# Thirty-two experts as one pipeline written in program order, a quarter of the weight subtractions on GpSimd

## The chip, the cores and the metric

The kernel runs on one core of a Trainium2 chip. The metric is the device time of one execution in microseconds (us), the median of several runs. Engines are named as the profile names them: PE (TensorE, matrix products), DVE (VectorE), ACT (ScalarE), POOL (GpSimd), SP (SyncE, which issues the loads).

## The reference

Three transformer blocks work one after the other on 512 tokens of 1024 features, in float32. The change touches only the third, and in it the mixture of experts:

```python
def clamped_swiglu_expert(xb, w_gu, b_gu, w_dn, b_dn):
    gu = xb @ w_gu + b_gu
    gate = jnp.minimum(gu[:, :D_FF_3], SWIGLU_LIMIT)
    up = jnp.clip(gu[:, D_FF_3:], -SWIGLU_LIMIT, SWIGLU_LIMIT)
    glu = gate * jax.nn.sigmoid(SWIGLU_ALPHA * gate)
    return ((up + 1.0) * glu) @ w_dn + b_dn
```

A router picks 4 of 32 experts for each token; each expert has 1024 x 2048 gate-and-up weights and 1024 x 1024 down weights, 12.58 MB together. The outputs of a token's four experts are summed, weighted by their gates. After the experts come a norm, a gate over a per-token embedding and a last norm.

## The kernel before

Blocks one and two fill the first 1900 us and stay as they are. In the third block `Moe.route` (L1423) finds each token's experts, and `Moe.run` (L1546) goes through the 32 experts. An expert has 96 slots (`CAP`) for its tokens.

**Exact products.** Every weight block, 128 x 2048 numbers (1 MB), is loaded by SP (`wblock`, L100, DMA at L92), copied by ACT into a rounded high part `wh` (L97), and DVE subtracts that from the block for a low part `wo` (L98). A product is then three matmuls (`mm3`, L163 to L167): high by high, high by low, low by high. An expert has 8 blocks of gate-and-up and 4 of down weights, each with 12 matmuls of 512 columns, so 144 matmuls, 12 copies on ACT and 12 subtractions on DVE. A load takes 512 columns of 512 rows of the matrix, so it reads runs of 2 KB.

**The rows of x.** `picked` (L1510) fetches and transposes an expert's tokens in one step: a matmul with a 0/1 matrix `hot` (L1516), for 3 experts at a time (`GRP`), over both parts of x, 64 matmuls per 3 experts. `places` (L1489) computes each slot's token, gate and target row, `chosen` (L1504) marks `hot` for a group.

**One expert.** `up` (L1610) opens an accumulator with the bias, a matmul over 64 rows (`bgu` has the two parts of the bias of 32 experts, L1617), then takes two blocks into it, and does this four times; `glu` (L1530) runs after each gate/up pair; `turn` (L1519) transposes a half of the hidden values; `down` (L1627) takes the four down blocks, ACT scales the result by the gate (L1639), and POOL adds the rows to the sum in DRAM by an indirect DMA (`add_rows`, L1722). Half 1 of an expert's `up` comes after the `down` of the one before. A scheduler orders the instructions of each engine.

**Buffers.** In the expert stage there are 5 tiles for loads, 3 for high parts, 3 for low parts. PSUM banks: 4 `gemm`, 3 `aux`, 1 `hold`.

**After the experts** `ple` (L1753) takes the sums back, with a bias matmul over 64 rows for each of 8 gate products (L1795).

Of the kernel before, what the change touches and what calls it, by code (L numbers as in the profile page):

```python
# [11 lines left out]
F32 = mybir.dt.float32  # L12
# [19 lines left out]
class Env:  # L32
    BANKS = {"gemm": 4, "aux": 3, "hold": 1}

    def __init__(self, ctx, tc):
        self.tc, self.nc = tc, tc.nc
        nc = self.nc
        self.cst = ctx.enter_context(tc.tile_pool(name="cst", bufs=1))
# [3 lines left out]
        self.psp = ctx.enter_context(tc.tile_pool(name="ps", bufs=4, space=bass.MemoryType.PSUM))  # L42
# [5 lines left out]
        self.n = 0  # L48
# [11 lines left out]
    def widen(self, ctx, slots, **more):  # L60
# [18 lines left out]

    def ps(self, s, tag="aux"):  # L80
# [24 lines left out]
    def split(self, hi, lo, src, scale=None):  # L105
        """src * scale into two float32r parts."""
# [8 lines left out]
    def bank(self, ctx, n):  # L115
        """n tiles [128, 4, 512] on the right until ctx closes."""
# [20 lines left out]
    def give(self, *tiles):  # L137
        """What was read for the last time."""
# [6 lines left out]
    def lend(self, n):  # L145
        """n more tiles each for the two parts of weights; returns what ends that."""
# [22 lines left out]
    def gemm_tok(self, xs, K, w, c0, cn, consume, eng=None):  # L169
        """Token-major: consume(tt, col, n, psum) for psum[tok, col:col+n] = x @ w[:, col:col+n]."""  # L170
# [52 lines left out]
    def bcast(self, pool, src, n, tag):  # L223
        """A row of n values in DRAM onto all partitions."""
# [4 lines left out]
    def transpose_in(self, xs, t, src, k=KT):  # L229
        """src [tok of tile t, k*128 features] into the feature-major pairs xs."""  # L230
# [8 lines left out]
    def rstd(self, pool, ssq, n, eps, tag):  # L239
        """(ssq / n + eps) ** -0.5 of a few columns."""  # L240
# [8 lines left out]
    def rms(self, pool, x, gain, eps, out, scratch=None):  # L249
        """out = x * rsqrt(mean(x^2) + eps) * gain of one token tile [128, 1024]."""  # L250
# [6 lines left out]
    def layer_norm(self, pool, x, eps, out, gain, bias, tag=""):  # L257
        """out = (x - mean) * rstd * gain + bias of one token tile [128, 1024]."""
# [17 lines left out]
def block1(e, a, res, more):  # L276
    """The first block's x, and what the second's first product takes."""
# [17 lines left out]
    with ExitStack() as ph:  # L295
# [8 lines left out]
        # -------- i_k, i_w, m_i, m_f in one stationary block  # L304
# [33 lines left out]
        # index keys: norm over the 64 features, on both partition halves  # L338
# [24 lines left out]
        # relative bias: strips of 256 keys per head, less the value of far keys  # L363
# [23 lines left out]
        # causal mask inside one tile of 128 keys: 0 where key <= query  # L387
# [11 lines left out]
        # -------- mLSTM gates, a head per partition  # L399
# [37 lines left out]
        # selectors of a head's row: pairs of 64 partitions, and all 128  # L437
# [9 lines left out]
        # token-major columns of c, the key weights and the floor of the denominator  # L447
# [11 lines left out]
        # 0 where key <= query within one chunk of 64, keys on partitions  # L459
# [39 lines left out]
        # -------- attention over the chosen keys, a head at a time, in three steps  # L499
# [50 lines left out]
        def attend(n0, n1):  # L550
            """Heads n0 to n1 of all 32, each step behind the one before it."""
# [11 lines left out]
        # -------- q, k of the mLSTM: causal conv over 4 tokens and silu  # L563
# [30 lines left out]
        # -------- mLSTM chunks  # L594
# [96 lines left out]
    # -------- ffn: conv of 3 tokens over both halves, silu(gate) * val  # L691
# [79 lines left out]
class Hidden:  # L771
    """Feature tiles [128, 512] of a ffn's hidden layer, four to a slot but the first ones."""
# [5 lines left out]
    def parts(self):  # L778
        """Of each slot: its first feature tile, how many, the slot."""
# [8 lines left out]
class Modulated:  # L788
    """layer_norm(x) * scale + shift, token tile by token tile, as a feature-major operand."""
# [13 lines left out]
class Ada:  # L803
    """silu(c) @ w_ada + b_ada, by columns of 512; the row goes to DRAM."""
# [34 lines left out]
def down(e, hd, w, add, done):  # L839
    """add(t, cols, psum) of hidden @ w, all eight accumulators open at once, then done(t)."""  # L840
# [41 lines left out]
def block2(e, a, u, res):  # L882
    """The second block's x, and the same feature-major, from e.xsp and its modulated norm u."""
# [5 lines left out]
    with ExitStack() as ph:  # L889
# [7 lines left out]
        # lower bounds: softmax over the two rows of logits, a head's features per column  # L897
# [16 lines left out]
        # 1 where key <= query within one chunk, keys on partitions  # L914
# [22 lines left out]
        for g in range(2):  # L937
# [35 lines left out]
            def prepare(j):  # L973
# [7 lines left out]
                # queries against the chunk's start and against their sub-chunk's  # L981
# [9 lines left out]
                # keys against each sub-chunk's start, and against the chunk's end  # L991
# [69 lines left out]
    with ExitStack() as ph:  # L1061
# [16 lines left out]
        # the first half where the gates of the first heads were  # L1078
# [33 lines left out]
        # -------- gates, projections, and the sum that w_out takes  # L1112
# [143 lines left out]
# tokens of an expert in the first pass, and experts whose tokens are picked at once  # L1256
# [15 lines left out]


def mixer3(e, a, x, xt, moe):
    """x = layer_norm(alpha * x + mixers), routed."""
    nc, tc = e.nc, e.tc
    with ExitStack() as ph:
# [3 lines left out]
        # taps and scales of a feature per partition  # L1281
# [586 lines left out]
```

## Time and profile before

| | |
|---|---|
| median of 3 runs | 3298.11 us (3297.29 to 3299.51) |
| the profiled execution: span of its instructions | 3294.7 us |
| PE busy, share of the span | 3222.8 us, 98% |
| DVE, ACT, POOL busy | 65%, 47%, 8% |
| DMA rate in the expert stage, GB/s | 307 to 363 by slices of 30 us |
| first bias matmul of expert 0 | 1939.35 us |
| last down matmul of expert 31 starts | 3206.79 us |

The span is the time from the first to the last instruction of the profiled execution, 3.4 us less than the median of the runs. Busy times of engines overlap; a busy engine is only the limit where it doesn't wait. A PE row's duration is longer than the distance to the next row, since matmuls are pipelined: the distance between starts is what a matmul costs.

### The profile page before, as it was taken

To read this page: it belongs to the slowest core of one execution; us is meant where nothing else is said; L and a number is where in the kernel's file an instruction comes from. 1 tells how busy PE (TensorE), PEld (TensorE's weight loads), DVE (VectorE), ACT (ScalarE), POOL (GpSimd) and SP (SyncE) were. 2 spreads that over 40 slices of the span, in tenths; PEclk is the share of its full clock that TensorE was granted. 3 is DMA by queue.
4 is the path that set the end of the run, shared out by engine and by line. 5 is a ranking of instruction groups with operands and counts; after the bars stand their busy time and mean duration, and the time that the engine had idled before them with its cause. 6 is when DMAs were issued, how large, how long until landed. Compare 5 with 4: busy or idle time off the path is not lost. (4 is left out here: it accounts for less than half of the span.)

```text
span 3294.7 us, 37481 instructions
## 1 busy us (share of the span) xinstructions
PE 3222.8 (98%) x15051; PEld 2434.6 (74%) x15051; DVE 2128.5 (65%) x2381; ACT 1564.5 (47%) x1655; POOL 272.7 (8%) x203
## 2 busy tenths in 40 slices
PE   7999999999999999999999999999999999999997
PEld 6776877878777788788778776666666666666665
DVE  5854687444636523822335778788888788888786
ACT  5343333323625223222322347777677667766662
POOL 2310011101000000200000100000000000000001
PEclk9997999999999999999999999999999999999999
DMA  4211465333222333232232259999999999999992
GB/s 143 77 39 62 147 218 201 115 109 97 64 64 64 89 113 122 87 109 92 83 119 90 91 204 330 332 324 319 330 329 329 327 327 325 323 331 325 328 328 104
DMA packets 324081, 626.96 MB, mean 190 GB/s; under 512 B 25144, under 2 KB 32672, under 8 KB 323834
## 3 DMA queue, kind: packets, MB, share of 16 engines
q1 hardware_dynamic: 320314, 611.89, 54.2%
q0 software_dynamic: 3584, 12.58, 1.9%
q8 instruction: 120, 1.97, 0.2%
q14 instruction: 63, 0.52, 0.0%
HBM read 603.43 MB, written 21.01 MB: 190 GB/s over the span
## 5 line engine op out<-in xcount | busy, mean ns | idle before, releaser
L98 DVE TENSOR_TENSOR wo<-wl,wh 128x2048 fp32r<-128x2048 f32 (+2 forms) x531 | 1190.3, 2254 | 627.8 <-ACT wh L97 625.8
L97 ACT ACTIVATE wh<-wl 128x2048 fp32r<-128x2048 f32 (+2 forms) x537 | 1009.0, 1885 | 744.6 <-PE pf L167 319.1
L165 PE MATMUL pf<-ah,wh 128*128 128x512 f32 (+1 forms) x1520 | 563.4, 371 | 0.6 <-ACT wh L97 0.6
L166 PE MATMUL pf<-ah,wo 128*128 128x512 f32 (+1 forms) x1520 | 562.2, 370 | 1.2 <-DVE wo L98 1.2
L167 PE MATMUL pf<-al,wh 128*128 128x512 f32 (+1 forms) x1520 | 561.5, 370 | 0.0
L165 PEld LDWEIGHTS pf<-ah,wh 128*128 128x128 f32 x1520 | 287.4, 189 | 56.4 <-ACT cy L727 6.9
L166 PEld LDWEIGHTS pf<-ah,wo 128*128 128x128 f32 x1520 | 287.0, 189 | 51.4 <-DVE wo L98 1.4
L167 PEld LDWEIGHTS pf<-al,wh 128*128 128x128 f32 x1520 | 286.5, 189 | 51.7 <-issue 3.7
L165 PE MATMUL pgu<-wh,xe 128*96 128x512 f32 x784 | 316.7, 404 | 0.0
L167 PE MATMUL pgu<-wo,xe 128*96 128x512 f32 x784 | 310.1, 396 | 1.8 <-DVE wo L98 1.7
L166 PE MATMUL pgu<-wh,xe 128*96 128x512 f32 x784 | 310.3, 396 | 0.0
L166 PE MATMUL pd<-wh,h 128*96 128x512 f32 x512 | 201.9, 394 | 0.0
L165 PE MATMUL pd<-wh,h 128*96 128x512 f32 x512 | 201.9, 394 | 0.0
L167 PE MATMUL pd<-wo,h 128*96 128x512 f32 x512 | 201.5, 393 | 0.1
L1722 POOL DMA_INDIRECT yd<-y,dst x32 | 79.1, 2472 | 1212.1 <-ACT y L1639 1112.1
L165 PEld LDWEIGHTS pgu<-wh,xe 128*96 128x96 f32 x784 | 126.3, 161 | 69.3 <-issue 22.2
L167 PEld LDWEIGHTS pgu<-wo,xe 128*96 128x96 f32 x784 | 126.6, 161 | 57.6 <-DVE wo L98 6.0
L166 PEld LDWEIGHTS pgu<-wh,xe 128*96 128x96 f32 x784 | 126.7, 162 | 45.9
L165 PE MATMUL pa<-wh,ah 128*128 128x512 f32 x352 | 143.0, 406 | 0.0
L167 PE MATMUL pa<-wo,ah 128*128 128x512 f32 x352 | 141.5, 402 | 0.2 <-DVE wo L98 0.2
L166 PE MATMUL pa<-wh,al 128*128 128x512 f32 x352 | 141.7, 402 | 0.0
L165 PE MATMUL pdn<-wh,ah 128*128 128x512 f32 x352 | 139.1, 396 | 0.7 <-ACT wh L97 0.7
(484 smaller groups left out, 4615.2 us busy)
## 6 DMA issues: line engine op xcount, KB each, us to landing
wl<-w_gate_up SPq DMA_DIRECT2D x256, 1024.0 KB
wl<-w_down SPq DMA_DIRECT2D x138, 1024.0 KB
wl<-w_in SPq DMA_DIRECT2D x54, 1024.0 KB
wl<-w_ada SPq DMA_DIRECT2D x24, 1024.0 KB
wl<-w_up SPq DMA_DIRECT2D x20, 1024.0 KB
wl<-w_ffn_in SPq DMA_DIRECT2D x20, 1024.0 KB
wl<-w_out SPq DMA_DIRECT2D x12, 1024.0 KB
wl<-w_ffn_out SPq DMA_DIRECT2D x10, 1024.0 KB
```

Of the source, the lines that this page charges most:

```text
L97: nc.scalar.activation(hi[:, :nk, :n], land[:, :nk, :n], AF.Copy)
L98: (eng or nc.vector).tensor_tensor(lo[:, :nk, :n], land[:, :nk, :n], hi[:, :nk, :n].bitcast(F32), op=ALU.subtract)
L165: mm(out, st[0], mv[0], start=first, stop=False)
L166: mm(out, st[1], mv[0], start=False, stop=False)
L167: mm(out, st[0], mv[1], start=False, stop=last)
L1722: self.e.nc.gpsimd.indirect_dma_start(out=self.yd, out_offset=bass.IndirectOffsetOnAxis(ap=dst[:, :1], axis=0), in_=y, in_offset=None, com ...
```

## The change

- The weights come in blocks of 128 whole rows (8 KB runs), the down weights by pairs of rows, also 8 KB; still 1 MB each. Loads are issued 7 blocks ahead, and copies and subtractions 3 blocks ahead (L1621 to L1630 of the changed kernel).
- Of the 12 subtractions of an expert, 9 stay on DVE and 3 go to POOL (`n % 4 == 1`, L1629): blocks 1 and 5 of gate-and-up and block 1 of down.
- A block now feeds all four gate/up accumulators, which are open together; their four bias matmuls (L1580) stand at the expert's start and use all 128 rows, as `sel` has zeros for the rest.
- `picked` is gone, and the two parts of x with it. `fetch` (L1549) computes the places and POOL gathers the 96 rows of x from DRAM by an indirect DMA (L1561), two experts ahead; `turn` transposes them, 8 more transposes per expert, with a copy on ACT and a subtraction on DVE for each four.
- The order is by program on every engine (`manual_schedule`): expert i's 8 wide blocks, the 4 narrow ones of expert i - 1, and so on; `glu` does both halves at once behind wide block 7.
- Rings: 5 tiles for loads, 4 high, 4 low. PSUM: 4 `gemm`, 2 `aux`, 2 `hold`. `ple` has its own pool, and its gate bias uses 128 rows.

```diff
-        self.sel = cp.tile([P, E], F32R, name="sel")
+        self.sel = cp.tile([P, E + 1], F32R, name="sel")
+        pick = tmp.tile([P, E + 1], F32, tag="pick", name="pick", bufs=1)
+        nc.gpsimd.memset(pick, 0.0)
...
     def room(self, ctx):
-        self.e.widen(ctx, 2, wh=1, wo=1)
+        self.e.widen(ctx, wl=2, wh=2, wo=2)
...
     def run(self, out):
...
+        e.layout(gemm=4, aux=2, hold=2)
...
+        def fetch(i):
...
+            pi, *took[i] = self.places(hots[p][:, :, j, :], self.tge[:, :, i, :])
+            src = wp.tile([P, 1], I32, tag="src", name=e.name("src"))[:CAP, :]
+            nc.vector.tensor_copy(src, pi[:, 0:1])
+            rows[i] = mp.tile([P, D], F32, tag="xg", name=e.name("xg"))[:CAP, :]
+            nc.gpsimd.indirect_dma_start(out=rows[i], out_offset=None, in_=self.xd,
+                                         in_offset=bass.IndirectOffsetOnAxis(ap=src[:, :1], axis=0))
...
+        def turn_x(i, g):
+            if i < N_EXP:
+                xs[i, g] = self.turn(rows[i][:, g * 512:(g + 1) * 512], entry("xe", 4))
+
+        def turn_h(i):
+            hs[i] = [self.turn(g, entry("h", 4), 1.0 / SW, 2) for g in gs.pop(i)]
+
+        def tops(i):
+
+            acc[i] = [e.ps("pgu", "gemm")[:CAP, :] for _ in range(4)]
+            for c in range(4):
+                nc.tensor.matmul(acc[i][c], self.sel[:, i:i + 1].to_broadcast([P, CAP]),
+                                 self.bgu[:, c * 512:(c + 1) * 512], start=True, stop=False)
+
+        def wide(i, k):
+            xh, xl = xs[i, k // 4]
+            hi, lo = tiles.pop(0)
+            for c in (0, 2, 1, 3):
+                e.mm3(acc[i][c], (xh[:, k % 4, :], xl[:, k % 4, :]), (hi[:, c, :], lo[:, c, :]), False, k == KT - 1)
...
+        def halve(n):
+            if n < len(steps):
+                land, hi, lo = lands.pop(0), e.ring("wh", F32R), e.ring("wo", F32R)
+                nc.scalar.activation(hi, land, AF.Copy)
+                eng = nc.gpsimd if n % 4 == 1 else nc.vector
+                eng.tensor_tensor(lo, land, hi.bitcast(F32), op=ALU.subtract)
+                tiles.append((hi, lo))
...
+        ahead, loaded = 3, 7
+        with tc.manual_schedule():
...
+            for n, (step, i, k, _) in enumerate(steps):
+                load(n + loaded)
+                halve(n + ahead)
+                if step is wide and k == 0:
+                    tops(i)
+                step(i, k)
+                if step is wide:
+                    if k == 2:
+                        fetch(i + 2)
+                    elif k in (4, 5):
+                        turn_x(i + 1, k - 4)
+                    elif k == KT - 1:
+                        gs[i] = self.glu(*[(acc[i][f], acc[i][2 + f]) for f in range(2)])
+                elif k == 3:
+                    ends(i)
+                    if i + 1 < N_EXP:
+                        turn_h(i + 1)
```

**PE, an expert's bias.** Here PE stands at an accumulator's bias in the kernel before (`pgu` is an accumulator, `xe` and `spot` hold rows of x, `pt` takes transposes):

```order
L167 MATMUL pgu_16253<-wo_16258,xe_15224 96x512
L165 MATMUL pgu_16253<-wh_16275,spot 96x512
L166 MATMUL pgu_16253<-wh_16275,spot 96x512
L1617 MATMUL pgu_16291<-bgu,sel 96x512
L1525 MATMUL pt_16336<-ident,g_16247 128x96 x4
L167 MATMUL pgu_16253<-wo_16276,spot 96x512
L165 MATMUL pgu_16253<-wh_16275,spot 96x512
```

and here at the start of an expert in the changed one:

```order
L1515 MATMUL pt_16364<-ident,g_16267 128x96 x4
L1580 MATMUL pgu_16377<-bgu,sel 96x512
L1580 MATMUL pgu_16378<-bgu,sel 96x512
L1580 MATMUL pgu_16379<-bgu,sel 96x512
L1580 MATMUL pgu_16380<-bgu,sel 96x512
L166 MATMUL pgu_16377<-wh_16299,xe_16195 96x512
L167 MATMUL pgu_16377<-wh_16299,xe_16195 96x512
L168 MATMUL pgu_16377<-wo_16300,xe_16195 96x512
L166 MATMUL pgu_16379<-wh_16299,xe_16195 96x512
```

The four bias matmuls stand in a row, a block's high part is then used for one accumulator after the other, and the picks of x (L1516) have gone from PE; four transposes stand in their place twice per expert.

**DVE, one expert.** In the kernel before DVE goes through an expert so (`g`, `u` are the gate products, `h` the transposed hidden values):

```order
L98 TENSOR_TENSOR wo_16349<-wl_16346,wh_16348 128x2048
L1538 TENSOR_SCALAR u_16332<-pgu_16291 96x512
L1539 SCALAR_TENSOR_TENSOR g_16329<-u_16332,g_16329 96x512
L98 TENSOR_TENSOR wo_16367<-wl_16364,wh_16366 128x2048
L98 TENSOR_TENSOR wo_16385<-wl_16382,wh_16384 128x2048
L98 TENSOR_TENSOR wo_16403<-wl_16400,wh_16402 128x2048
L113 SCALAR_TENSOR_TENSOR h_16421<-pt_16422,h_16421 128x384
L98 TENSOR_TENSOR wo_16476<-wl_16473,wh_16475 128x2048
L98 TENSOR_TENSOR wo_16494<-wl_16491,wh_16493 128x2048
```

and in the changed one, from `fetch`'s places to the gate products:

```order
L1498 TENSOR_TENSOR dst_16442<-free_16440,pi_16433 96x1
L1559 CAST src_16444<-pi_16433 96x1
L1629 TENSOR_TENSOR wo_16451<-wl_16333,wh_16450 128x2048
L1629 TENSOR_TENSOR wo_16469<-wl_16371,wh_16468 128x2048
L111 TENSOR_TENSOR xe_16484<-pt_16485,xe_16484 128x384
L1629 TENSOR_TENSOR wo_16495<-wl_16397,wh_16494 128x2048
L111 TENSOR_TENSOR xe_16510<-pt_16511,xe_16510 128x384
L1629 TENSOR_TENSOR wo_16539<-wl_16448,wh_16538 128x2048
L1527 TENSOR_SCALAR g_16554<-pgu_16377 96x512
L1527 TENSOR_SCALAR g_16556<-pgu_16378 96x512
L1532 TENSOR_SCALAR u_16560<-pgu_16379 96x512
```

The first subtraction here is wide block 6's, the one behind the second transposed half of x (`xe`, L111) narrow block 2's; those of wide block 5 and narrow block 1, which come just before them in the program, are POOL's. `glu`'s six instructions stand together, and two of them (L1534) read two operands from SBUF, as every subtraction does.

**POOL, the expert stage.** Before, POOL has one instruction per expert, the indirect add (L1722). In the changed kernel a stretch of it reads (`xg` are gathered rows, `yd` the sums):

```order
L1747 DMA yd<-y_14324,dst_13333 640x1024
L1629 TENSOR_TENSOR wo_14391<-wl_14288,wh_14390 128x2048
L1561 DMA xg_14419<-x3d,src_14417 96x1024
L1629 TENSOR_TENSOR wo_14494<-wl_14388,wh_14493 128x2048
L1629 TENSOR_TENSOR wo_14580<-wl_14491,wh_14579 128x2048
L1747 DMA yd<-y_14613,dst_13546 640x1024
L1629 TENSOR_TENSOR wo_14680<-wl_14577,wh_14679 128x2048
```

Per expert POOL now has three subtractions of a block, a gather and the add.

## Rows read from the trace of the kernel before

**Rows 1.** A stretch of the expert stage: us of stretch, busy us by engine, PEclk, DMA share, GB/s.

```profile
2400.00:2500.00 100.00, 99.58 (x448) 67.91 (x447) 82.38 (x60) 69.73 (x56) 5.09 (x2) 1.00 0.96 324
```

**Rows 2.** Waits, 2300 to 2700 us: us in total, times, longest.

```profile
DVE g L1535 <- PE pgu L167: 27.9, 20, 2.0
PE pgu L167 <- DVE wo L98: 1.4, 7, 0.2
```

**Rows 3.** PE's timeline from the routing to the first expert: start, duration, what.

```profile
1939.35 0.47 PE L1617 MATMUL pgu<-bgu,sel 64*96 64x512 f32 x1
```

**Rows 4.** PE's timeline at the end of the expert stage.

```profile
3207.02 0.60 PE L1414 MATMUL pz<-ident,pt 128*128 128x128 f32 x4
```

**Rows 5.** PE's timeline inside one expert.

```profile
2401.55 0.39 PE L165 MATMUL pgu<-wh,xe 128*96 128x512 f32 x1
...
2406.20 0.40 PE L167 MATMUL pgu<-wo,spot 128*96 128x512 f32 x1
2406.53 0.47 PE L1617 MATMUL pgu<-bgu,sel 64*96 64x512 f32 x1
...
2407.24 0.39 PE L166 MATMUL pgu<-wh,xe 128*96 128x512 f32 x1
...
2422.22 0.49 PE L1525 MATMUL pt<-ident,g 96*128 96x96 f32 x4
2422.49 1.17 PE L1516 MATMUL pt<-spot,xs 128*128 128x288 f32 x7
2423.50 0.40 PE L167 MATMUL pd<-wo,h 128*96 128x512 f32 x1
```

**Rows 6.** POOL's timeline: two subtractions of a block (L98), two gate products (L1336).

```profile
52.42 5.49 POOL L98 TENSOR_TENSOR wo<-wl,wh 128x2048 fp32r<-128x2048 f32 x1 [8.68 <-ACT wh L97]
...
93.48 4.63 POOL L98 TENSOR_TENSOR wo<-wl,wh 128x2048 fp32r<-128x2048 f32 x1 [24.26 <-ACT wh L97]
...
1851.95 1.41 POOL L1336 TENSOR_TENSOR cy<-cy,bg 128x512 f32<-128x512 f32 x1 [2.55 <-ACT wh L97]
1854.84 3.20 POOL L1336 TENSOR_TENSOR cy<-cy,bg 128x512 f32<-128x512 f32 x1 [1.48 <-DVE cy L1334]
```

**Rows 7.** DVE's timeline beside those instructions of POOL.

```profile
53.58 4.35 DVE L419 TENSOR_TENSOR ml<-gl,g 4x8 f32<-4x8 f32 x1
...
1852.12 0.68 DVE L1331 TENSOR_TENSOR cg<-cg,pf 128x512 f32<-128x512 f32 x1
...
1854.61 2.28 DVE L98 TENSOR_TENSOR wo<-wl,wh 128x2048 fp32r<-128x2048 f32 x1
1856.81 2.61 DVE L110 TENSOR_TENSOR al<-cy,ah 128x512 fp32r<-128x512 f32 x2
```

**Rows 8.** DVE's timeline inside one expert.

```profile
2452.90 0.69 DVE L1535 TENSOR_SCALAR g<-pgu 96x512 f32<-96x512 f32 x1 [1.19 <-PE pgu L167]
2453.51 0.54 DVE L113 SCALAR_TENSOR_TENSOR h<-pt,h 128x384 fp32r<-128x384 f32 x1
2453.97 2.28 DVE L98 TENSOR_TENSOR wo<-wl,wh 128x2048 fp32r<-128x2048 f32 x1
```

**Rows 9.** A group of instructions by line, 2000 to 3200 us: busy us, mean ns.

```profile
L1507 DVE TENSOR_TENSOR spot<-slot,pos 128x1152 fp32r<-128x1152 f32 x9 | 12.1, 1345 | 0.0
```

**Rows 10.** A stretch with the DMA queue full.

```profile
3160.00:3165.00 5.00, 4.87 (x24) 3.31 (x23) 4.93 (x3) 3.10 (x3) 0.00 (x0) 1.00 1.05 397
```

**Rows 11.** DVE's timeline: the last token tile's places are known.

```profile
1929.51 0.22 DVE L1454 SCALAR_TENSOR_TENSOR pos<-pp,mask 128x32 f32<-128x32 f32 x1 [2.22 <-PE pp L1453]
```

**Rows 12.** DMA issues, 2000 to 3200 us: times, median us to landing.

```profile
yd<-y,dst POOLq DMA_INDIRECT x30, 9.6
```

**Rows 13.** A stretch behind an idle PE.

```profile
3210.00:3215.00 5.00, 5.00 (x16) 3.94 (x15) 1.78 (x2) 2.19 (x3) 0.00 (x0) 0.66 1.07 347
```

**Rows 14.** PE's timeline in that stretch.

```profile
3209.44 0.50 PE L165 MATMUL pa<-wh,p 128*128 128x512 f32 x1 [1.82 <-ACT wh L97]
...
3211.20 0.63 PE L167 MATMUL pa<-wo,p 128*128 128x512 f32 x1
```

More of the change, by code (lines that the diff above doesn't have):

```diff
@@ L78, in name, with layout @@
         return f"{s}_{self.n}"
+    def layout(self, **banks):
+        self.BANKS = banks
+        self.psx.close()
+        self.psp = self.psx.enter_context(self.tc.tile_pool(name=self.name("ps"), bufs=4, space=bass.MemoryType.PSUM))
     def ps(self, s, tag="aux"):
@@ L1468, in route @@
         e.split(self.tge[:, t, :, 2], self.tge[:, t, :, 3], ge)
-        e.split(*[h[t // 2].rearrange("p (h a) n -> p h (a n)", h=2)[:, t % 2, :] for h in self.xs], x[:, t, :])
         if 0 < t < NT - 1:
@@ L1483, in routed @@
         nc.vector.tensor_copy(self.count[:, E:], most)
-    def share(self):
-        self.xs = [[self.e.slot("xs", F32R, 0) for _ in range(NT // 2)] for _ in range(2)]
     def places(self, hot, tge):
@@ L1508, in chosen, with turn @@
                                        pos.rearrange("p e t -> p t e")[:, :, :, None].to_broadcast(shape), op=ALU.is_equal)
-    def picked(self, hot, f, part, out, copy, tag):
-        e, nc = self.e, self.e.nc
-        pt = e.ps("pt", tag)[:, :GRP * CAP]
-        for t in range(NT):
-            x = self.xs[part][t // 2].rearrange("p (h a) n -> p h (a n)", h=2)[:, t % 2, f * P:(f + 1) * P]
-            nc.tensor.matmul(pt, x, hot[:, t].rearrange("p e s -> p (e s)"), start=t == 0, stop=t == NT - 1)
-        copy(out, pt)
-    def turn(self, src, both, scale=None):
+    def turn(self, src, both, scale=None, step=1):
         e, nc = self.e, self.e.nc
@@ L1607, in run @@
-        e.give(self.xs)
-        self.ple(out)
-    def up(self, i, xs, f):
-        e, nc = self.e, self.e.nc
-        w = self.a["w_gate_up_3"][0, i]
-        acc = []
-        for c in (f * 512, D + f * 512):
-            p = e.ps("pgu", "gemm")[:CAP, :]
-            nc.tensor.matmul(p, self.sel[:2 * N_EXP, i:i + 1].to_broadcast([2 * N_EXP, CAP]), self.bgu[:2 * N_EXP, c:c + 512],
-                             start=True, stop=False)
-            for k0 in (0, 4):
-                hi, lo = e.wblock(w, k0, 4, c, 512, hold=None if i or f or c == 0 and k0 == 0 else self.pos1[:, 0, NT - 1:])
-                xh, xl = xs[k0 // 4]
-                for k in range(4):
-                    e.mm3(p, (xh[:, k, :], xl[:, k, :]), (hi[:, k, :], lo[:, k, :]), False, k0 + k == 7)
-            acc.append(p)
-        return self.glu(*acc)
@@ L1627, in down @@
[L1627 to L1640 removed]
+        e, nc, tc, wp = self.e, self.e.nc, self.e.tc, self.wp
@@ new lines, in wide, with narrow @@
+        def wide(i, k):
[3 more added lines that the diff above has]
+                e.mm3(acc[i][c], (xh[:, k % 4, :], xl[:, k % 4, :]), (hi[:, c, :], lo[:, c, :]), False, k == KT - 1)
+        def narrow(i, j):
+            if j == 0:
+                acc[i] = [e.ps("pd", "hold")[:CAP, :] for _ in range(2)]
+            hi, lo = tiles.pop(0)
+            hh, hl = hs[i][j // 2]
+            for f in range(2):
+                for k in range(2):
+                    q = j % 2 * 2 + k
+                    e.mm3(acc[i][f], (hh[:, q, :], hl[:, q, :]), (hi[:, 2 * k + f, :], lo[:, 2 * k + f, :]),
+                          j + k == 0, j == 3 and k == 1)
@@ new lines, in ends @@
+        def ends(i):
+            y = wp.tile([P, D], F32, tag="y", name=e.name("y"))[:CAP, :]
+            gate, dst = took.pop(i)
+            for f in range(2):
+                nc.scalar.activation(y[:, f * 512:(f + 1) * 512], acc[i][f], AF.Copy, scale=gate)
+            self.add_rows(dst, y)
+        steps = []
+        for i in range(N_EXP + 1):
+            if i < N_EXP:
+                w = self.a["w_gate_up_3"][0, i]
+                steps += [(wide, i, k, w[k * P:(k + 1) * P, :]) for k in range(KT)]
+            if i:
+                w = self.a["w_down_3"][0, i - 1]
+                steps += [(narrow, i - 1, j, w[j * 256:(j + 1) * 256, :].rearrange("(p i) n -> p (i n)", i=2)) for j in range(4)]
@@ new lines, in run @@
+        mark(0)
+        fetch(0)
+        self.biased(NT - 2)
+        self.biased(NT - 1)
+        fetch(1)
+        self.routed()
+        for g in range(2):
+            turn_x(0, g)
+        ahead, loaded = 3, 7
+        with tc.manual_schedule():
+            for n in range(loaded):
+                load(n)
+                if n - (loaded - ahead) >= 0:
+                    halve(n - (loaded - ahead))
+            for n, (step, i, k, _) in enumerate(steps):
[15 more added lines that the diff above has]
+                        turn_h(i + 1)
+                if step is wide and (i, k) == (1, 1):
+                    turn_h(0)
@@ L1642, in crowded @@
+        ph.close()
+        self.ple(out)
     def crowded(self, out):
@@ L1753, in ple, with ended @@
     def ple(self, out):
+        with self.e.tc.tile_pool(name=self.e.name("pl"), bufs=1) as lp:
+            self.ended(out, lp)
+    def ended(self, out, lp):
         e, nc, a, wp = self.e, self.e.nc, self.a, self.wp
@@ L1816, in ple @@
         last(NT - 1)
-        e.give(own)
 def rel_hot():
```

151 lines of the change are left out of this document (51 added, 100 removed).

## The prediction

> **What bounds the kernel now.** I read the expert stage by stretches first: the reader is to see PE busy for 99.58 of 100 us at the full clock (1.00), DVE for 82, ACT for 70, POOL for 5, and the DMA engines for 0.96 at 324 GB/s [rows 1]. The waits then say which of the two full ones, PE or DMA, ends last: in 400 us PE waits 1.4 us for a weight block, while DVE waits 27.9 us for PE at the first gate product alone, 20 times, 1.4 us each [rows 2]. So PE sets the pace, DMA is just behind. The stage runs from the first bias at 1939.35 [rows 3] to 3207.02, where the last down matmul gives way to the next stage [rows 4]: 1267.7 us, 39.6 us per expert. That is the number to change; the rest of the kernel only at its two seams.
>
> PE's 39.6 can be built from its timeline [rows 5]. Twenty plain steps lie between 2401.55 and 2406.20, so a 512-column matmul costs 0.2325 us; 144 of them, 33.5. A bias lies between 2406.20 and 2407.24, where two plain steps would take 0.47: it costs 0.57, four of them (one is the row at 2406.53) 2.3. Four transposes take 0.27 (2422.22 to 2422.49), two sets 0.5. Seven picks take 1.01, so 0.144 each; 64 per three experts, 3.1 per expert. With four small matmuls for the places, at the price of four transposes, that is 39.7.
>
> **PE after.** The picks go (-3.1), 8 transposes of gathered rows come (+0.5). The 128-row bias has no row; its ends are 0.2325, a plain matmul of 128 rows and 512 columns, and 0.57, today's. I take the lower, as four now stand together and nothing in them differs from a plain one: 0.9 instead of 2.3. PE then needs 33.5 + 0.9 + 1.1 + 0.3 = 35.8 us, 37.1 at the other end. If PE still set the pace, 32 x 3.8 = 122 us would be gone.
>
> **What is late next: the subtractions.** POOL takes three of twelve. Alone, one lasts 4.63 us there [rows 6], 2.28 on DVE [rows 7]. Busy time is then no obstacle: POOL 13.9 plus two indirect DMAs. But the rows show the two engines shutting each other out. POOL's subtraction at 52.42 ends at 57.91; DVE's tiny product of 4 x 8 elements, begun at 53.58, lasts 4.35 us and ends at 57.93 [rows 6, 7]. The other way, POOL's gate product takes 1.41 alone, but 3.20 at 1854.84, where a DVE subtraction runs undisturbed from 1854.61 for 2.28 [rows 6, 7]. Not every DVE instruction does it: at 1852.12 a product with one operand from PSUM takes its 0.68 beside a POOL product of 1.41. So I take it that a DVE instruction with two SBUF operands and a POOL one exclude each other for their whole length.
>
> The Trainium skill, page "SBUF — State Buffer", section "Who interferes with whom", says the same of DVE instructions with two SBUF inputs beside a GpSimd instruction that reads SBUF, and that the second to start fully blocks. By that rule the sum is the one below; without it, PE's 35.8 would stand.
>
> The chain of exclusive work per expert: nine subtractions on DVE at 2.20, from one start to the next (1854.61 to 1856.81 [rows 7]), 19.8; three on POOL, 13.9; two products of `glu` (L1534) at 0.61, from one start to the next [rows 8], 1.2; a third of the marking at 1.345 [rows 9], 0.4. Together 35.3. DVE has also four clips from PSUM at 0.61 (2.4), four subtractions of transposes at 0.46 (1.8, from 2453.51 to 2453.97 [rows 8]), and four one-column instructions, 0.3 by estimate, below the 0.46. As DVE takes its instructions in order, these 4.6 lengthen the chain except where they stand directly behind a subtraction that is POOL's. By the order of the change that is so for the places (0.3) and one half of x (0.46). So 35.3 + 4.6 - 0.8 = **39.1 us per expert**, against 39.6: 32 x -0.5 = -16 us. PE then waits some 3.3 us per expert.
>
> **DMA.** It moves 12.58 MB of weights, 0.39 gathered and 0.39 added. At today's 324 GB/s with 0.96 of the engines' time [rows 1], all of it would be 338, so 13.36 MB take 39.5 us; at the 397 GB/s of a full queue [rows 10], 33.6. Runs of 8 KB instead of 2 KB are a quarter of the packets; I take the lower end, as even 2 KB runs reach it. It lies under the chain then. ACT, busy for 70 of 100 us [rows 1], loses its copies of the picks and gets two of transposes per expert; it stays hidden.
>
> **Seams.** At the start the picks (until 1939) go, but now places must be known (1929.5 [rows 11]), the group marked (1.3), places summed (1.0, an estimate), rows gathered, transposed and split (1.3 from [rows 5, 8]). A gather isn't shown; the add by the same kind of DMA lands after 9.6 us [rows 12], which is the upper end, a quarter of it the lower. With 9.6: 1942.7, +3 (-4 to +5 with a colder PE). At the end eight gate biases save 0.34 each, 2.7, and the last transposes of hidden values are no longer covered, +1.3. Together +2.
>
> The order the change writes leaves no freedom for a scheduler, so that it does what it says is hardly in doubt.
>
> **Sum.** -16 + 2 = -14. The profiled span of 3294.7 becomes 3281; runs have a median 3.4 us above it, so from the median of 3298.1: **3284 us**. Its own ends: 39.9 per expert if none of the 0.8 overlaps, +10 + 2, 3310; 37.9 if two of the four clips run beside POOL too (1.2 less), -54 + 2, 3246.
>
> **Rivals.**
> 1. *No exclusion worth the name*, as POOL's three fall into gaps of DVE, which waits for PE anyway [rows 2]. Then PE's 35.8 stands: -122 + 2, **3178 us**. For it: DVE's own 9 subtractions and other work are 26 of 39.6 us, so there are gaps. Against: 13.9 us of POOL would need such gaps in pieces of 4.63, and DVE, three blocks ahead, has none by order. Chance 0.20.
> 2. *The chain is longer than an expert is now*: slower. Place: DVE's queue at wide block 7, where `glu`'s first clip waits for PE to finish all four accumulators, and narrow block 3's subtraction and all later ones wait behind it. Before, this wait (1.4 us each [rows 2]) cost nothing. If nothing of the 0.8 overlaps and half of one such wait enters the chain once per expert, it is 39.9 + 0.7 = 40.6: +32 + 2, **3332 us**; with the whole wait 41.3, 3354. It decides as soon as the chain passes 39.6. What makes it worse is PE's clock: behind an idle time of 1.82 us PE went on at a mean granted 0.66 [rows 13], with plain matmuls of 0.63 instead of 0.39 at one point [rows 14], that is at the lower of its two levels, 1.2 GHz. If PE idles in pieces of that length, its 35.8 grow too: at 0.24 for each of a dozen matmuls, 3 us. For it: four accumulators end together, so DVE's wait is for all of them. Chance 0.28.
> 3. *8 KB runs bring nothing*: DMA at 39.5 us is the pace, 39.6 - 39.5 gives -3, with the seams **3297 us**. For it: 0.96 of the engines' time was full before. Against: the full queue's 397 GB/s. Chance 0.05.
>
> **How the numbers follow.** The forecast has 0.47. Differences under 0.2% (6.6 us) can't be told from none by a measurement of this kernel. Of the forecast's 0.47, 0.32 lies below 3291.5, 0.10 within, 0.05 above; rival 1 is faster, rival 2 slower, rival 3 mostly within. Faster 0.53, same 0.14, slower 0.33. The range must reach rival 1 at 3178, and rival 2's 3332 with something towards 3354: **3172 to 3345**. The forecast's own range is 3246 to 3310.
>
> **What would show it.** Exclusion: in the expert stage POOL's L1629 lasts over 5 us, or DVE's L1629 has a mean well above 2.28, each ending where the other engine's ends; PE waits for the low part (`wo`), its busy share falls to about 0.92. Bias: L1580 rows 0.23 apart. DMA: a share under 0.95 with 340 GB/s. Rival 1: DVE's subtraction stays at 2.28, POOL's at 4.63, PE is full. Rival 2: PEclk under 1.00 in the stage, DVE idle behind PE at L1527. The forecast is wrong if an expert takes under 38 or over 40 us.

## The result and the profile after

The changed kernel takes 3330.28 us (3323.60 to 3330.94, 4 runs) where the one before took 3297.7 in the same comparison: the ratio is 1.0094 (95% interval 1.0080 to 1.0108). It is 33 us slower. The forecast was 3284, faster; the range reached 3345, and rival 2 had 3332.

The profiled execution has a span of 3327.9 us, 33.2 more than before, so the profile shows the whole difference. The same stretch of the expert stage as [rows 1] (us of stretch, busy us of PE, PEld, DVE, ACT, POOL, then PEclk, DMA share, GB/s):

```profile
2400.00:2500.00 100.00, 94.79 (x430) 66.64 (x429) 93.90 (x60) 68.83 (x53) 53.92 (x13) 0.98 0.91 340
```

PE is busy for 94.8 us where it was 99.6, its granted clock is 0.98 and was 1.00, DVE has 94 and POOL 54 instead of 82 and 5, and DMA's share falls to 0.91 at a higher rate. The waits between 2300 and 2700 us (total, times, longest), against [rows 2]:

```profile
DVE wo L1629 <- ACT wh L1627: 33.8, 25, 2.5
...
PE pd L168 <- DVE wo L1629: 14.2, 10, 3.3
PE pgu L168 <- DVE wo L1629: 14.2, 6, 2.4
```

PE now waits 28.4 us for low parts made by DVE, in 16 waits of up to 3.3 us; it was 1.4 us in 7. No wait of PE for a low part made by POOL is in the list. DVE's wait for PE at the first clip, which [rows 2] shows, is gone from the list; DVE waits for ACT's high parts instead, 3.4 us per expert. The groups by line, 2000 to 3200 us (busy us, mean ns), show what has become longer:

```profile
L1629 DVE TENSOR_TENSOR wo<-wl,wh 128x2048 fp32r<-128x2048 f32 x267 | 888.0, 3353 | 112.8 <-ACT wh L1627 109.2
L1629 POOL TENSOR_TENSOR wo<-wl,wh 128x2048 fp32r<-128x2048 f32 x90 | 458.4, 5093 | 470.9 <-ACT wh L1627 461.2 <-PE pgu L167 7.1 <-PE pgu L168 2.7
...
L1504 DVE TENSOR_TENSOR hot<-slot,pos 128x1152 fp32r<-128x1152 f32 x9 | 27.9, 3095 | 0.0
```

DVE's subtraction has a mean of 3.35 us (2.28 alone [rows 7]), POOL's 5.09 (4.63 alone [rows 6]), the marking of a group 3.10 (1.35 in [rows 9]). One collision in DVE's timeline and POOL's:

```profile
2399.05 4.66 DVE L1629 TENSOR_TENSOR wo<-wl,wh 128x2048 fp32r<-128x2048 f32 x1 [2.49 <-ACT wh L1627]
...
2434.39 6.68 DVE L1629 TENSOR_TENSOR wo<-wl,wh 128x2048 fp32r<-128x2048 f32 x1
```

```profile
2396.95 4.61 POOL L1629 TENSOR_TENSOR wo<-wl,wh 128x2048 fp32r<-128x2048 f32 x1 [2.85 <-ACT wh L1627]
...
2434.26 4.66 POOL L1629 TENSOR_TENSOR wo<-wl,wh 128x2048 fp32r<-128x2048 f32 x1 [3.86 <-ACT wh L1627]
```

POOL's subtraction runs from 2396.95 to 2401.56. DVE's next one starts at 2399.05 and needs 2.28; it lasts 4.66, that is until 2.2 us behind POOL's end. At 2434.26 and 2434.39 the two start almost together: POOL takes its 4.66, DVE 6.68.

The time of an expert is read from one start of its bias matmuls to the next; three in a row in PE's timeline:

```profile
2413.04 1.15 PE L1580 MATMUL pgu<-bgu,sel 128*96 128x512 f32 x4
...
2454.30 1.15 PE L1580 MATMUL pgu<-bgu,sel 128*96 128x512 f32 x4
...
2491.63 1.15 PE L1580 MATMUL pgu<-bgu,sel 128*96 128x512 f32 x4
```

41.3 us, then 37.3. From the second expert's start (1973.69) to the last one's (3185.54) it is 40.4 on average, mostly 37.3, 39.9 or 41.4. Before it was 39.6. So it is over the 40 from which on the prediction called itself wrong.

### The profile page after: what moved, and what is told of

Its sections match the earlier page's. It is cut to its first block, busy times and chain, and to the rows that moved or that the text cites. A ratio compares the mean times of both kernels' runs of the same rounds, so it can differ in the third digit from the quotient of the medians.

```text
span 3327.9 us, 36769 instructions
## 1 busy us (share of the span) xinstructions
PE 3157.5 (95%) x14603; PEld 2392.9 (72%) x14603; DVE 2246.5 (68%) x2365; ACT 1518.3 (46%) x1547; POOL 905.0 (27%) x333
## 5 line engine op out<-in xcount | busy, mean ns | idle before, releaser
L1629 DVE TENSOR_TENSOR wo<-wl,wh 128x2048 fp32r<-128x2048 f32 x288 | 945.6, 3309 | 129.1 <-ACT wh L1627 125.3
L1627 ACT ACTIVATE wh<-wl 128x2048 fp32r<-128x2048 f32 x384 | 725.2, 1912 | 164.0 <-PE pgu L167 104.3
L99 DVE TENSOR_TENSOR wo<-wl,wh 128x2048 fp32r<-128x2048 f32 (+2 forms) x147 | 320.9, 2186 | 543.3 <-ACT wh L98 534.6
L1629 POOL TENSOR_TENSOR wo<-wl,wh 128x2048 fp32r<-128x2048 f32 x96 | 486.8, 5071 | 531.0 <-ACT wh L1627 521.3
L98 ACT ACTIVATE wh<-wl 128x2048 fp32r<-128x2048 f32 (+2 forms) x153 | 277.5, 1817 | 621.1 <-PE pf L168 320.9
L168 PE MATMUL pgu<-wo,xe 128*96 128x512 f32 x1024 | 413.9, 404 | 47.9 <-DVE wo L1629 47.9
L166 PE MATMUL pgu<-wh,xe 128*96 128x512 f32 x1024 | 416.9, 407 | 0.0
L167 PE MATMUL pgu<-wh,xe 128*96 128x512 f32 x1024 | 412.1, 402 | 0.0
L167 PEld LDWEIGHTS pgu<-wh,xe 128*96 128x96 f32 x1024 | 170.0, 166 | 68.1 <-issue 1.2
L166 PEld LDWEIGHTS pgu<-wh,xe 128*96 128x96 f32 x1024 | 170.1, 166 | 66.3 <-issue 0.9
L168 PEld LDWEIGHTS pd<-wo,h 128*96 128x96 f32 x512 | 84.7, 165 | 87.2 <-DVE wo L1629 51.1
L1561 POOL DMA_INDIRECT xg<-x3d,src x32 | 126.4, 3948 | 72.8 <-DVE src L1559 54.7
```

The costliest lines, as they stand in the source:

```text
L98: nc.scalar.activation(hi[:, :nk, :n], land[:, :nk, :n], AF.Copy)
L99: (eng or nc.vector).tensor_tensor(lo[:, :nk, :n], land[:, :nk, :n], hi[:, :nk, :n].bitcast(F32), op=ALU.subtract)
L166: mm(out, st[0], mv[0], start=first, stop=False)
L167: mm(out, st[1], mv[0], start=False, stop=False)
L168: mm(out, st[0], mv[1], start=False, stop=last)
L1561: nc.gpsimd.indirect_dma_start(out=rows[i], out_offset=None, in_=self.xd, in_offset=bass.IndirectOffsetOnAxis(ap=src[:, :1], axis=0))
```

## The experiments

Theory A: DVE's and POOL's subtractions exclude each other, and that chain sets the pace. Theory B: POOL is merely slow, its three blocks come late. Theory C: the rest of the change (order, gather, 8 KB runs) costs the time. Times of the kernel before in these comparisons were 3298 to 3300 us.

**1. All subtractions on DVE.**

```diff
-                eng = nc.gpsimd if n % 4 == 1 else nc.vector
+                eng = nc.vector
```

> The changed kernel with all twelve subtractions of an expert on DVE, none on POOL. Theory A (DVE and POOL shut each other out, and that chain of 40.5 us per expert is the pace): DVE's subtractions go back from a mean of 3.35 us to about 2.29, PE sets the pace at 35.8 us per expert, 32 x 4.7 = 150 us less than the changed kernel, about 3180 us (3170 to 3205), with the clock at 1.00 in the stage. Theory B (POOL is only slow: the three blocks it makes come late, DVE has time to spare): DVE now has 12 x 2.2 + 6 = 33 us of work in 35.8, so also near 3180; it parts from A in the run with the spare subtractions. Theory C (program order, gather or 8 KB runs are what costs): 3280 or more.

Measured: 3190.34 us (3187.07 to 3192.31), 0.967 of the kernel before (0.9654 to 0.9686), 140 us less than the change. The stretch from 2400 to 2500 us:

```profile
2400.00:2500.00 100.00, 100.00 (x470) 71.50 (x469) 91.46 (x71) 73.77 (x56) 20.61 (x6) 1.00 0.98 367
```

DVE's group by line, 2000 to 3050 us:

```profile
L1629 DVE TENSOR_TENSOR wo<-wl,wh 128x2048 fp32r<-128x2048 f32 x350 | 790.8, 2288 | 83.1 <-ACT wh L1627 77.3
```

PE is busy for 100 of 100 us at the full clock, DVE's mean is 2.29, an expert takes 36.1 us. Theory C falls: without POOL's share everything else in the change is worth 108 us. A and B both stand.

**2. One subtraction of twelve on POOL.**

```diff
-                eng = nc.gpsimd if n % 4 == 1 else nc.vector
+                eng = nc.gpsimd if n % 12 == 1 else nc.vector
```

> The changed kernel with one subtraction of twelve on POOL (wide block 5). Theory A: the exclusive chain is 11 x 2.2 + 4.6 + 1.6, with 4.6 of DVE's other work 35.0 us, just under PE's 35.8: 3180 to 3200 us. Theory B: one late block instead of three, a third of the loss: about 3230 us. Theory C: 3280 or more.

Measured: 3194.10 us (3188.55 to 3200.90), a ratio of 0.9688 (0.9669 to 0.9708). The groups of DVE and POOL:

```profile
L1629 DVE TENSOR_TENSOR wo<-wl,wh 128x2048 fp32r<-128x2048 f32 x320 | 754.6, 2397 | 42.0 <-ACT wh L1627 37.8
L1629 POOL TENSOR_TENSOR wo<-wl,wh 128x2048 fp32r<-128x2048 f32 x29 | 134.6, 4641 | 139.1 <-ACT wh L1627 139.1
```

A's number, not B's: one collision per expert lengthens DVE's mean to 2.40 and is hidden under PE's 36.1. POOL does take work off DVE (754.6 us of subtractions where run 1 has 790.8 in the same stretch), but there is nothing to win by it where PE is the pace.

**3. Spare subtractions on POOL that nobody waits for.**

```diff
+        dup = mp.tile([P, 4, 512], F32, tag="dup", name="dup", bufs=1)
+        nc.gpsimd.memset(dup, 0.0)
...
-                eng = nc.gpsimd if n % 4 == 1 else nc.vector
+                eng = nc.vector
+                if n % 4 == 1:
+                    nc.gpsimd.tensor_tensor(dup, dup, dup, op=ALU.subtract)
```

> All twelve subtractions on DVE, and beside them POOL makes three spare ones per expert on a tile of its own, which nobody reads and nobody waits for. Theory A: the chain is 12 x 2.2 + 13.9 + 1.6 + 4.6 = 46.5 us per expert at most, less what falls into DVE's waits: 3400 to 3530 us, DVE's subtractions far over 2.29 us. Theory B (late results of POOL): same as with all twelve on DVE alone, about 3180, since no result of POOL is waited for.

Measured: 3432.37 us (3429.82 to 3434.38), a ratio of 1.0408 (1.0391 to 1.0426). Groups:

```profile
L1633 DVE TENSOR_TENSOR wo<-wl,wh 128x2048 fp32r<-128x2048 f32 x330 | 1033.7, 3179 | 3.0
L1632 POOL TENSOR_TENSOR dup<-dup 128x2048 f32<-128x2048 f32 x82 | 362.7, 4423 | 3.1
L168 PE MATMUL pd<-wo,h 128*96 128x512 f32 x448 | 199.7, 446 | 131.9 <-DVE wo L1633 131.6
```

This settles A against B: no result of POOL is used here, and 242 us are lost. POOL's spare instructions have a mean of 4.42 us, DVE's go from 2.29 to 3.18, and PE waits 132 us for DVE at the down products alone.

**4. Spare memsets in the same places.** The diff is that of run 3 with `nc.gpsimd.memset(dup, 0.0)` for the subtraction.

> As the run before, but POOL's spare work is a memset of 128 x 2048, which reads nothing from SBUF. Theory A as the rows bear it out (two operands read on one side, a read on the other): no exclusion, time as with all twelve on DVE, about 3180. If any SBUF access of POOL shuts DVE out: longer by up to 3 x 2 us x 32 = 190 us; DVE's subtractions lengthened.

Measured: 3192.36 us (3187.53 to 3196.14), as in run 1. Groups:

```profile
L1633 DVE TENSOR_TENSOR wo<-wl,wh 128x2048 fp32r<-128x2048 f32 x349 | 788.7, 2289 | 82.9 <-ACT wh L1629 76.5 <-PE pgu L168 0.9
L1632 POOL MEMSET dup<- 128x2048 f32 x87 | 172.4, 1982 | 1.8
```

POOL writes the same 128 x 2048 numbers for 1.98 us each, every one of the 87 memsets overlaps a subtraction of DVE, by 1.5 us on average, and DVE's mean stays at 2.29. So neither POOL's presence nor its writes shut DVE out; what run 3's instruction has beyond a memset is that it reads its operands.

**5. The kernel before with 128-row biases alone.** `sel` gets its zeros as in the change, and L1617 and L1795 use all rows:

```diff
-            nc.tensor.matmul(p, self.sel[:2 * N_EXP, i:i + 1].to_broadcast([2 * N_EXP, CAP]), self.bgu[:2 * N_EXP, c:c + 512],
+            nc.tensor.matmul(p, self.sel[:, i:i + 1].to_broadcast([P, CAP]), self.bgu[:, c:c + 512],
```

> The kernel before with one thing of the change: the bias matmuls (four per expert, eight behind the experts) over 128 rows, zeros in the added ones. Theory: a 128-row bias costs a plain matmul, 0.2325 us instead of 0.57, and PE sets the pace: (4 x 32 + 8) x 0.34 = 46 us less, 3252. Rival: the price is that of any matmul on another operand behind a series, and 128 rows change nothing: 3298. DMA, at 0.96 of its time, may take part of the gain back: 3260 to 3280.

Measured: 3257.61 us (3253.50 to 3258.53), a ratio of 0.9876 (0.9859 to 0.9892): 41 of the 46 us.

The same stretch of this run:

```profile
2400.00:2500.00 100.00, 99.62 (x478) 72.46 (x477) 84.26 (x61) 72.91 (x64) 7.64 (x3) 1.00 0.99 344
```

DMA's share has gone from 0.96 to 0.99 here. But the list of this run's waits, 2300 to 2700 us, has none for a load, so DMA isn't shown to have kept the last 5 us; where they went stays open.

**6. Biases of 64 rows, but four in a row,** in the kernel of run 1: `self.sel[:64, ...]` and `self.bgu[:64, ...]` in `tops`.

> All twelve subtractions on DVE, as in the first run, but the four bias matmuls of an expert over 64 rows. If the rows count: four of 64 rows in a row cost one or two changes of 0.34 us rather than four, 0.3 to 1.4 us per expert, 10 to 44 us more than the first run's 3190. If only standing apart counts: no change.

Measured: 3199.45 us (3195.84 to 3207.82), 9 us more than run 1, a ratio of 0.9699 (0.9682 to 0.9715) to the kernel before. PE's timeline of run 1 (128 rows), then of this run (64):

```profile
2187.00 1.08 PE L1515 MATMUL pt<-ident,g 96*128 96x96 f32 x8
2187.87 1.14 PE L1580 MATMUL pgu<-bgu,sel 128*96 128x512 f32 x4
2188.85 0.40 PE L166 MATMUL pgu<-wh,xe 128*96 128x512 f32 x1
2189.08 0.40 PE L167 MATMUL pgu<-wh,xe 128*96 128x512 f32 x1
```

```profile
2230.12 1.08 PE L1515 MATMUL pt<-ident,g 96*128 96x96 f32 x8
2231.14 1.16 PE L1580 MATMUL pgu<-bgu,sel 64*96 64x512 f32 x4
2232.22 0.47 PE L166 MATMUL pgu<-wh,xe 128*96 128x512 f32 x1
2232.53 0.40 PE L167 MATMUL pgu<-wh,xe 128*96 128x512 f32 x1
```

From the transposes in front of the biases to the first product's second step it is 2.08 us with 128 rows (2187.00 to 2189.08) and 2.41 with 64 (2230.12 to 2232.53). So 0.33 is paid once for the change to 64 rows and back, not per bias: 32 x 0.33 = 11 us. The pace agrees: an expert takes 36.4 us here and 36.1 in run 1, from the fourth expert on. The Trainium skill, page "TensorEngine Tiling (Array Packing)", section "Tiling Modes", says that changing the tiling mode drains the engine; the rows agree, with 0.33 us for a change and the one back.

**7. 2 KB runs in the kernel of run 1.**

```diff
-                nc.sync.dma_start(land.rearrange("p a b -> p (a b)"), steps[n][3])
+                for c in range(4):
+                    nc.sync.dma_start(land[:, c, :], steps[n][3][:, c * 512:(c + 1) * 512])
```

> All twelve subtractions on DVE, as in the first run, but every weight block loaded by four DMAs of 2 KB runs instead of one of 8 KB runs. If 2 KB runs are held to the kernel before's rate (324 GB/s at a share of 0.96, 338 at most): 13.36 MB take 39.5 us per expert, 3.4 us more than now, about 3300 us. If the run length doesn't matter (397 GB/s in a full queue before): 3190.

Measured: 3287.74 us (3282.97 to 3296.49, 10 runs), 97 us more than run 1, a ratio of 0.9975 (0.9965 to 0.9985) to the kernel before.

The same stretch:

```profile
2400.00:2500.00 100.00, 95.95 (x435) 67.31 (x434) 84.44 (x67) 67.48 (x53) 13.76 (x6) 0.97 1.02 336
```

Waits, 2300 to 2700 us:

```profile
ACT wh L1628 <- DMA wl<-w_gate_up: 34.4, 19, 4.0
```

DMA is full, a share of 1.02 at 336 GB/s, and ACT's copies wait for loads. So these loads give 336 / 1.02 = 329 at a full share in this stretch; run 1's stretch, where PE sets the pace, has 367 at 0.98. Whole rows in one load carry 97 us of run 1's gain: without them DMA holds the stage at 39.3 us per expert. But the edit changes two things, the runs (2 KB) and the size of a DMA (four of 256 KB for one of 1 MB). In run 5 loads of 1 MB with 2 KB runs move 344 GB/s at 0.99, 347 at a full share, which lies between; how much of the 97 us is the run length and how much the size of a DMA is not shown.

**8. Zero matmuls into PE's waits.** The changed kernel, with a zero column in `sel` and one matmul by it ahead of each block but one:

```diff
+        def nothing(out):
+            nc.tensor.matmul(out, self.sel[:, N_EXP + 1:].to_broadcast([P, CAP]), self.bgu[:, :512], start=False, stop=False)
...
             hi, lo = tiles.pop(0)
+            nothing(acc[i][0])
             for c in (0, 2, 1, 3):
...
             hh, hl = hs[i][j // 2]
+            if j:
+                nothing(acc[i][0])
```

PE's timeline of the changed kernel, behind its longest wait in an expert, was the reason to try it:

```profile
2441.12 0.47 PE L168 MATMUL pd<-wo,h 128*96 128x512 f32 x1 [3.31 <-DVE wo L1629]
...
2442.99 0.63 PE L166 MATMUL pd<-wh,h 128*96 128x512 f32 x1
2443.42 0.63 PE L167 MATMUL pd<-wh,h 128*96 128x512 f32 x1
...
2446.47 0.39 PE L166 MATMUL pd<-wh,h 128*96 128x512 f32 x1
```

PE waits 3.31 us, goes on with steps of 0.23 (rows left out), and 1.5 us later falls to steps of 0.43, at the lower of its clock's two levels (1.2 GHz), until 2446. Adding up PE's steps over ten experts, from 2294.7 to 2697.3, six have such a slow stretch, 1.4 to 1.6 us each in excess of 0.2325 a step: 0.9 us per expert.

> The changed kernel (three subtractions per expert on POOL) with eleven added matmuls per expert that add zero, one ahead of a block: 2.6 us more work for PE, in the place where it waits 3.3 us per expert now. Theory: the pace of 40.45 is 39.5 in which DVE or POOL's subtraction is busy, and 0.95 in which PE, at the lower clock behind its waits, holds the chain up; with the waits filled the clock stays up and 32 x 0.95 = 30 us go, 3300 us. Rival: the clock drops cost nothing, as PE has slack: 3330. Rival: PE's work counts in full: 3330 + 82 = 3412.

Measured: 3290.11 us (3284.60 to 3292.99, 10 runs), a ratio of 0.9972 (0.9962 to 0.9981): 40 us less than the changed kernel, by adding work.

The same stretch:

```profile
2400.00:2500.00 100.00, 99.44 (x461) 70.61 (x460) 93.22 (x61) 69.10 (x54) 54.69 (x13) 1.00 0.91 338
```

PE's wait that is left, 2300 to 2700 us:

```profile
PE pd L168 <- DVE wo L1635: 2.4, 4, 0.6
```

The clock is at 1.00, PE's waits are 2.4 us in 400, and an expert takes 38.7 us, or 39.5 where a group is marked, 39.0 on average. But 38.7 is also what PE needs here, 36.1 + 11 x 0.2325, so this run doesn't say how short the chain is; run 11 does.

**9. The control: the same zero matmuls with all subtractions on DVE.** The diff is that of runs 1 and 8 together.

> The control for the added zero matmuls: the same eleven per expert, but all twelve subtractions on DVE, where PE never waits. Theory: PE's work counts in full where PE sets the pace, 11 x 0.2325 x 32 = 82 us more than the first run's 3190, 3272 us, the clock at 1.00 in both. Rival: the added matmuls change the time in some other way (a better order, a slot that was idle): less than 40 us more.

Measured: 3269.50 us (3263.27 to 3274.13), a ratio of 0.9909 (0.9892 to 0.9926): 79 us more than run 1. The matmuls cost their full price where PE sets the pace, so run 8 wins by having them where PE waits. That they act there by the clock, and not by shifting when the engines meet, these two runs can't tell; rows of the changed kernel under "Why the prediction was wrong" can, for the larger part.

**10. The kernel before with three subtractions on POOL.**

```diff
-                hi, lo = e.wblock(w, k0, 4, c, 512, hold=...
+                hi, lo = e.wblock(w, k0, 4, c, 512, eng=nc.gpsimd if c >= D and k0 else None, hold=...
-                hi, lo = e.wblock(w, k0, 4, f * 512, 512)
+                hi, lo = e.wblock(w, k0, 4, f * 512, 512, eng=nc.gpsimd if k0 and not f else None)
```

> The kernel before with one thing of the change: three of an expert's twelve subtractions on POOL, under its own scheduler, 2 KB runs and picks. Theory A (exclusion): nine subtractions on DVE at 2.2, three on POOL at 4.63, two products and what DVE does besides make 39 to 40 us, about PE's 39.6; with collisions in bad places and waits of PE 3300 to 3400 us, DVE's subtractions with a mean over 2.6 us. If POOL's part ran in parallel, PE's 39.6 would stand: 3298.

Measured: 3382.60 us (3381.57 to 3384.28), a ratio of 1.0253 (1.0236 to 1.0270). Groups:

```profile
L98 DVE TENSOR_TENSOR wo<-wl,wh 128x2048 fp32r<-128x2048 f32 x255 | 665.5, 2622 | 205.8 <-ACT wh L97 204.5
L98 POOL TENSOR_TENSOR wo<-wl,wh 128x2048 fp32r<-128x2048 f32 x86 | 434.2, 5048 | 500.2 <-ACT wh L97 470.9 <-PE pgu L167 29.3
L167 PE MATMUL pd<-wo,h 128*96 128x512 f32 x448 | 178.2, 398 | 26.7 <-POOL wo L98 26.7
```

The instructions are lengthened as in the change. But the number alone isn't A's here: PE waits for POOL's blocks, not DVE's, and DVE stands idle for 206 us. In this order, with three high and three low parts, B's mechanism is there as well; in the changed order PE waits for a block of POOL's once, 0.6 us, from 1990 to 3200 us, and run 3 loses its time without using any.

**11. Six zero matmuls instead of eleven.** As run 8, but only in wide blocks 1, 3, 5, 7 and narrow blocks 1 and 3:

```diff
-            nothing(acc[i][0])
+            if k % 2:
+                nothing(acc[i][0])
...
-            if j:
+            if j % 2:
```

> Run 8 with six zero matmuls per expert instead of eleven (wide blocks 1, 3, 5, 7 and narrow blocks 1, 3). In run 8 an expert takes 38.7 us, and PE's own need is there 36.1 + 11 x 0.2325 = 38.7: if PE sets the pace and the exclusive chain is shorter than that once PE doesn't stumble, PE's need falls to 37.5 and the time by 32 x 1.2 = 37 us to 3253. If the chain is 38.7 to 39 by itself: 3290 as in run 8. If six are too few to keep the clock up: between 3290 and 3330, with a granted clock under 1.00 in the stage.

Measured: 3281.42 us (3278.79 to 3285.53), a ratio of 0.9952 (0.9935 to 0.9968).

The same stretch:

```profile
2400.00:2500.00 100.00, 97.76 (x453) 69.14 (x454) 93.17 (x59) 69.52 (x53) 64.51 (x14) 1.00 0.94 340
```

PE's wait for DVE, 2300 to 2700 us:

```profile
PE pd L168 <- DVE wo L1636: 10.4, 10, 1.6
```

PE needs 37.5 us per expert here and has waits again, 10.4 us in 400 and none above 1.6; the clock is at 1.00 in this stretch. An expert takes 38.9 us on average. So neither the first nor the second expectation alone: with PE out of the way the chain sets the pace, at 38.9. DVE or a subtraction on POOL is busy for all but 0.13 us of an expert, on the average of twenty. It is 49 us less than the changed kernel, with the same subtractions on the same engines.

## Why the prediction was wrong

**What failed** is the step from the chain to the pace: "PE then waits some 3.3 us per expert", with nothing charged for it. The waits came nearly as said, 28.4 us in ten experts. But out of most of its waits of 2.3 to 3.3 us PE falls to the lower clock, and the step took it for an engine with slack, to which a wait costs nothing. Of the 29 experts from 2014 to 3186 us, 19 have a slow stretch like the one shown under run 8 (three of them behind a wait of 1.6 us), 27.6 us in excess of 0.2325 a step, so 0.95 per expert and 32 x 0.95 = 30 us.

That such a stretch costs an expert its full length, two experts of the changed kernel show, those that start at 2491.63 and at 2574.54. In both PE waits 2.4 us for the low part of the same wide block; behind the first wait the clock falls, behind the second it doesn't (rows of PE, ACT and DVE, the first expert above):

```profile
2507.04 0.47 PE L168 MATMUL pgu<-wo,xe 128*96 128x512 f32 x1 [2.41 <-DVE wo L1629]
2507.68 0.63 PE L167 MATMUL pgu<-wh,xe 128*96 128x512 f32 x1
...
2510.99 0.49 PE L1515 MATMUL pt<-ident,xg 96*128 96x96 f32 x4
...
2511.52 0.49 ACT L110 ACTIVATE xe<-pt 128x384 fp32r<-128x384 f32 x1 [5.29 <-PE pt L1515]
...
2513.85 2.29 DVE L1629 TENSOR_TENSOR wo<-wl,wh 128x2048 fp32r<-128x2048 f32 x1 [1.25 <-ACT wh L1627]
```

```profile
2589.93 0.47 PE L168 MATMUL pgu<-wo,xe 128*96 128x512 f32 x1 [2.40 <-DVE wo L1629]
...
2592.32 0.49 PE L1515 MATMUL pt<-ident,xg 96*128 96x96 f32 x4
...
2592.86 0.49 ACT L110 ACTIVATE xe<-pt 128x384 fp32r<-128x384 f32 x1 [4.08 <-PE pt L1515]
...
2595.18 2.29 DVE L1629 TENSOR_TENSOR wo<-wl,wh 128x2048 fp32r<-128x2048 f32 x1
```

From the end of the wait to the transposes of x it is 3.95 us in the first and 2.39 in the second. ACT's copy of the transposes comes as much later, ACT makes its next high part only behind that copy, and DVE waits 1.25 us for the high part where in the second expert it doesn't wait. The first expert takes 41.5 us, the second 39.9. Run 11 has the same once more: of its experts with a marking, the two with a slow stretch take 41.1 us, the others 39.6 to 39.7.

Runs 8, 9 and 11 agree: matmuls that compute nothing take 40 and 49 us off the changed kernel, where PE waits, and add 79 where it doesn't. Of the 1.5 us per expert that run 11 wins, 0.8 is time in which neither DVE nor a subtraction on POOL is busy (0.95 in the changed kernel, 0.13 in run 11, averages of twenty experts). Not all of that is the clock's: of the two experts above the first has 2.06 us of such time and the second, with no slow stretch, still 0.59. The other 0.7 is that the busy time itself falls, from 39.45 to 38.75; why it falls is not shown, the two engines may meet in better places.

**The chain itself** was 39.1 in the sum, and the pace is 38.9 in run 11, where PE's clock is held and PE doesn't set it. In the changed kernel as it is, the time in which DVE or a subtraction on POOL is busy, added up from the two timelines, is 37.2 to 41.2 in ten experts, 39.5 on average: the same work, 0.35 longer than the sum had it. The marking is the plainest case, 0.4 per expert in the sum from 1.35 alone, and 3.10 there, shut out by POOL.

**The seams** were +2. Rows of PE there, the first transposes of gathered rows, the second expert's biases, and the stage's end:

```profile
1942.70 1.52 PE L1515 MATMUL pt<-ident,xg 96*128 96x96 f32 x8
...
1973.69 2.54 PE L1580 MATMUL pgu<-bgu,sel 128*96 128x512 f32 x4 [4.42 <-DVE g L1527]
1976.03 0.63 PE L166 MATMUL pgu<-wh,xe 128*96 128x512 f32 x1
...
3243.79 0.60 PE L1417 MATMUL pz<-ident,pt 128*128 128x128 f32 x4
```

The transposes start at 1942.70, when the prediction had them done and split, so 1.3 us later than forecast, and the end is at 3243.79, from where it takes 84.1 us to the span's end instead of 87.7: -3.6 for the biases and what follows. What was missed: between the first two experts there is no narrow block, so the second one's accumulators wait 4.42 us for the first one's `glu`, and PE goes on at the lower clock. Of the span's 33.2 us, 32 x (40.4 - 39.6) = 26 are pace and some 7 seams, where -16 and +2 stood: 42 and 5 us off, about the distance from 3284 to 3330. Of the 42, some 30 are the 0.95 us per expert in which neither engine subtracts, and 11 the chain's 0.35.

**Point by point.** Exclusion: right for the subtractions (run 3), but the prediction had it for any instruction of POOL beside a DVE one with two SBUF operands, and a memset on POOL does nothing to DVE (run 4). PE's own need of 35.8: 36.1 in run 1. The bias at a plain matmul's price: right, 41 of 46 us in the kernel before, and four in a row take 0.98 us. DMA: with 8 KB runs 367 GB/s at a share of 0.98, 374 at a full one, so 13.36 MB take 35.7 us, between the two ends; it was under the chain, as said, and rival 3, with DMA as the pace at 39.5 us, is refuted by run 1, where an expert takes 36.1. Rival 1 would have been the result without POOL: 3190 against its 3178.

**Rival 2** gave 3332 and had the right side, but not by its mechanism. It let DVE wait for PE at `glu`'s first clip; no such wait is in the list. Its remark on PE's clock, priced at 3 us, was the part that came true, at half of that in the experts that have it. So that its 3332 lies next to the measured 3330 is luck.

## What to carry to other kernels

Work moved from DVE to POOL runs beside it only where the two kinds of instruction don't shut each other out: subtractions of two SBUF operands on both engines are one queue, here 2.2 and 4.6 us in turn, and their sum must be set against the pace, not each engine's busy share. An engine that gets slack still isn't free to wait: PE's waits of 2.3 to 3.3 us here mostly brought it 1.3 to 1.6 us of loss at the lower clock afterwards, so a chain a little shorter than PE's old pace came out slower. The rest of the change, whole rows per load, four accumulators on one block and biases of 128 rows, is worth 108 us once the subtractions stay on DVE: 3190 us, the fastest kernel of this study.

## What the runs showed that was not expected

Six matmuls per expert that compute nothing made the changed kernel 49 us faster (run 11). A change to 64 rows and back costs PE 0.33 us with four matmuls between (run 6), as much as with one in the kernel before (0.34). And loads of 1 MB move more at the same share of DMA's time with 8 KB runs than with 2 KB runs: 367 GB/s at 0.98 (run 1) against 344 at 0.99 (run 5).
